# Normalising three of four query blocks' probabilities inside the transposing product

## The chip, the cores and the metric

The kernel runs on one core of one Trainium2 chip. The time is the device time in microseconds (us) of one execution. The kernel before took 2144.35 us (median of three runs, 2143.05 to 2144.57). The profile that is shown comes from one further execution, which took 2142.89 us and whose span, from its first to its last instruction, is 2141.1 us.

In the profile, PE is the matrix engine (TensorE), PEld its loading of the stationary operand, DVE the vector engine, ACT the scalar engine, POOL GpSimd and SP the engine that issues most DMAs. A name such as L855 is a line of the kernel before.

## The reference

Two layers, each with three token mixers that read the same normalised input of 1024 tokens: a gated delta rule, multi-head attention with latent projections, and a gated linear recurrence. The change lies in the attention alone, which is causal and swept over blocks of 128 queries, for 8 heads:

```python
def one_block(args):
    qi, i = args
    s = jnp.einsum('bhqd,bhkd->bhqk', qi, k).astype(jnp.float32) * scale
    qpos = i * Q_BLOCK + jnp.arange(Q_BLOCK)
    s = jnp.where(kpos[None, :] <= qpos[:, None], s, -jnp.inf)
    p = jax.nn.softmax(s, axis=-1).astype(v.dtype)
    return jnp.einsum('bhqk,bhkd->bhqd', p, v)
```

So each row of probabilities is exp(s - max) divided by its sum, and then multiplied with the values. All data are float32.

## The kernel before

Each layer has two stages. The first (`phase_a` and `lru`) holds the input projection and the two recurrent mixers. The second, `phase_c`, holds the attention and the projection of its output. Most products of the kernel are made of three single passes on operands that are split into a high and a low part of a rounded type (`mm3`, L132 to L136; the products at L805 to L809 and L866 to L868 are written out in the same manner). A few products, such as L392 and L379 of the first stage and the sums of squares at L209, work on unsplit float32 operands instead.

In `phase_c` each head's queries are taken in two halves (`sb` 0 and 1) of four blocks (`qi` 0 to 3). For each half two generators run:

- `attn_scores` forms for each query block the scores against all keys up to its own block, in one or two pieces of up to 512 keys (L805 to L809, in PSUM). DVE masks the diagonal block and takes the negative maximum (L815), ACT takes the exponential and its row sums (L823, recorded under the helper's L86) into a tile `P` of 512 or 1024 columns, DVE adds the sums and takes the reciprocal into `mx[:, 5:6]` (L826). Then the whole row of probabilities is multiplied by it: for `qi` 0 to 2 by POOL (the helper `gts`, L105), for `qi` 3 by DVE for the first 512 columns (L830) and by POOL for the other 512 in the second half.
- `attn_out` walks over the key blocks `kb`. For each it transposes the 128x128 blocks of the four (in the causal corner fewer) query blocks into one PSUM bank `tp` (L855), ACT rounds the bank into `th` (recorded as pth, L140) and DVE takes the rest `tl` (ptl, L141), and PE multiplies both with the values (L866 to L868). The products on one key block are issued after the transposes of the next one. There are two `tp` banks and two `th` and `tl` buffers.

The transposing is itself a product on PE: the block of `P` is the stationary operand and an identity matrix (`con`) the moving one. Counted over heads, halves and layers there are 576 of these: (10 + 26) per head, times 8 heads and 2 layers. Of them 384 belong to `qi` 0 to 2 (6 in the first half of a head, 18 in the second) and 192 to `qi` 3 (4 and 8).

The order of the work in `phase_c` is set in two steps: a list `todo` of generator steps with due times (in units of one half of a head), which puts a half's `attn_out` one unit after its `attn_scores` with a lag of 0.1, and mixes projections in between; and then the framework's scheduler, which orders each engine's queue by priority and its own estimate of durations. Engines then work through their queues in order.

Of the kernel before, what the change touches and what calls it, by code (L numbers as in the profile page):

```python
# [63 lines left out]
class Trunk:  # L64
# [718 lines left out]
    def attn_scores(self, h, sb, q, qr, k, P):  # L783

        nc, pc, con = self.nc, self.pc, self.con
        qh, ql = q[sb]
        qr = qr[h % 2]
        for qi in range(4):
            qb = sb * 4 + qi
            qs = slice(qi * 128, qi * 128 + 128)  # L790
            w = 128 * (qb + 1)

            pieces = [(0, w)] if w <= H2 else [(0, H2), (H2, w)]
            n = len(pieces)
            mx = pc.tile([128, 8], F32, name="mx", tag="mx", bufs=6)
            S = []
            for j, (k0, k1) in enumerate(pieces):
                ps = self.pb.tile([128, H2], F32, name="pS", tag="S")
                a = k0
                while a < k1:  # L800
                    e = min(k1, (a // H2 + 1) * H2)
                    kh, kl = k[a // H2]
                    ks = slice(a % H2, (e - 1) % H2 + 1)
                    out = ps[:, a - k0 : e - k0]
                    nc.tensor.matmul(out, qh[:, qs], kh[:, ks], start=True, stop=False)  # L805
                    nc.tensor.matmul(out, qh[:, qs], kl[:, ks], start=False, stop=False)
                    nc.tensor.matmul(out, ql[:, qs], kh[:, ks], start=False, stop=False)
                    nc.tensor.matmul(out, qr[sb][:, qs], self.kp[:, a:e], start=False, stop=False)
                    nc.tensor.matmul(out, qr[sb][:, qs], self.kl[:, a:e], start=False, stop=True)  # L809
                    a = e  # L810
                if j == n - 1:
                    dg = ps[:, k1 - k0 - 128 : k1 - k0]
                    self.tt(dg, dg, con[:, K_CAUS : K_CAUS + 128], ALU.add)
                S.append(ps[:, : k1 - k0])
                nc.vector.tensor_reduce(mx[:, j : j + 1], S[j], AX.X, ALU.max, negate=True)  # L815
            sc = self.scq[:, qb : qb + 1]
            if n == 2:
                nc.vector.tensor_scalar(mx[:, 2:3], mx[:, 0:1], mx[:, 1:2], sc, ALU.min, ALU.mult)  # L818
            else:
                nc.vector.tensor_scalar(mx[:, 2:3], mx[:, 0:1], sc, None, ALU.mult)  # L820
            pt = self.pp.tile([128, 512 * (sb + 1)], F32, name="P", tag=f"P{2 * (sb + 1)}", bufs=4)
            for j, (k0, k1) in enumerate(pieces):
                self.act(pt[:, k0:k1], S[j], AF.Exp, scale=sc, bias=mx[:, 2:3], accum_out=mx[:, 3 + j : 4 + j])  # L823
            if n == 2:
                nc.vector.tensor_scalar(mx[:, 3:4], mx[:, 3:4], mx[:, 4:5], None, ALU.add)
            nc.vector.reciprocal(mx[:, 5:6], mx[:, 3:4])  # L826
            if qi == 3:

                w0 = pieces[0][1]
                nc.vector.tensor_scalar(pt[:, :w0], pt[:, :w0], mx[:, 5:6], None, ALU.mult)  # L830
                if n == 2:
                    self.gts(pt[:, w0:w], pt[:, w0:w], mx[:, 5:6])
            else:
                self.gts(pt[:, :w], pt[:, :w], mx[:, 5:6])
            P.append(pt)
            yield

    def attn_out(self, h, sb, P, V, ops):

        nc, pc = self.nc, self.pc  # L840
        if sb == 0:
            ops.extend(pc.tile([128, T], F32R, name="o", tag="ob", bufs=6) for _ in range(2))
        oh, ol = ops
        s = slice(sb * H2, (sb + 1) * H2)
        mz = pc.tile([128, H2], F32, name="mz", tag="mzh", bufs=1)
        nc.sync.dma_start(mz, self.mzd[h][:, s])
        po = self.bank("po")
        nkb = 4 * sb + 4
        prev = None
        for kb in range(nkb + 1):  # L850
            if kb < nkb:
                q0 = max(0, kb - 4 * sb)
                tp = self.bank("tp")
                for qi in range(q0, 4):
                    nc.tensor.transpose(tp[:, qi * 128 : qi * 128 + 128], P[qi][:, kb * 128 : kb * 128 + 128], self.ident)  # L855
                th = pc.tile([128, H2], F32R, name="pth", tag="pth", bufs=2)
                tl = pc.tile([128, H2], F32R, name="ptl", tag="ptl", bufs=2)
                w = slice(q0 * 128, H2)
                self.split(th[:, w], tl[:, w], tp[:, w])
                here = (kb, w, th, tl)  # L860
            if prev:
                j, w, th, tl = prev
                vh, vl = V[j // 2]
                v0 = (j % 2) * 256 + (h % 2) * 128
                vs = slice(v0, v0 + 128)
                nc.tensor.matmul(po[:, w], vh[:, vs], th[:, w], start=(j == 0), stop=False)  # L866
                nc.tensor.matmul(po[:, w], vl[:, vs], th[:, w], start=False, stop=False)
                nc.tensor.matmul(po[:, w], vh[:, vs], tl[:, w], start=False, stop=(j == nkb - 1))  # L868
            prev = here
            if kb < nkb:  # L870
                yield
        self.gate_split(po, 0.5, mz, oh[:, s], ol[:, s], nc.gpsimd)
# [376 lines left out]
```

## Time and profile before

| | |
|---|---|
| median of three runs | 2144.35 us |
| the profiled execution | 2142.89 us |
| its span | 2141.1 us |
| PE busy | 2052.8 us, 96% of the span |
| PE's weight loads (PEld) busy | 1686.7 us, 79% |
| DVE, ACT, POOL busy | 60%, 39%, 32% |
| attention of the first layer, about | 700 to 1040 us |
| attention of the second layer, about | 1755 to 2100 us |
| transposes of P (L855), 576 records | 98.6 us busy |
| POOL's normalising of P (L105), 112 instructions | 80.3 us busy |

Busy times are unions of records, and PE's records overlap: a matmul's record ends well after the next one has started. What a matmul costs PE in a row of them is therefore read from the distance of starts and not from its own duration.

### The profile page before, as it was taken

Reading aid. Unit: us, or ns where it says so; the run is one execution under the profiler, and the core shown is the slowest. Engines: PE = TensorE matmul, PEld = TensorE weight load, DVE = VectorE, ACT = ScalarE, POOL = GpSimd, SP = SyncE. Lnnn points to the kernel's source line nnn. Section 1 sums busy time; section 2 is a strip of 40 time slices with the busy share of each in tenths; the row PEclk is TensorE's granted clock in tenths of the full one; section 3 lists DMA queues with packets and bytes.
Section 4 is the critical chain, followed back from the end, with each engine's and each line's share of the span. In section 5 each row is a group of like instructions: output and inputs, shape, how many; then the busy total and the mean of one; then the engine's idle time right before and its main releaser. Section 6 shows DMA issues by size and latency. Waiting matters only on the chain.

```text
span 2141.1 us, 28752 instructions
## 1 busy us (share of the span) xinstructions
PE 2052.8 (96%) x10380; PEld 1686.7 (79%) x10380; DVE 1289.3 (60%) x2530; ACT 841.9 (39%) x1759; POOL 676.6 (32%) x752
## 2 busy tenths in 40 slices
PE   7999999999999999999899999999999989999997
PEld 4888878787777788888678888787877878888875
DVE  6556546544831777676754575474458237776766
ACT  5241243144720554443542313432366125444534
POOL 2132332233241433332332223333223423332322
PEclk9999999999999999999999999999999999999999
DMA  5123113414143015335511321134232520335263
GB/s 176 55 81 116 55 50 104 123 55 143 45 173 131 25 50 177 110 119 180 189 54 40 114 86 52 60 104 133 69 108 79 177 92 24 110 119 164 65 216 123
DMA packets 135103, 222.08 MB, mean 104 GB/s; under 512 B 37808, under 2 KB 60336, under 8 KB 134960
## 3 DMA queue, kind: packets, MB, share of 16 engines
q1 hardware_dynamic: 134960, 220.24, 31.6%
q8 instruction: 82, 1.34, 0.3%
q14 instruction: 61, 0.50, 0.1%
HBM read 147.31 MB, written 72.88 MB: 103 GB/s over the span
## 4 chain that ended last, share of the span: by engine, by line
PE 83%; DVE 6%; ACT 4%; DMA 3%; issue 2%; POOL 2%; SPq 0%; DVEq 0%; POOLq 0%; ACTq 0%
PE pbig L136 12%; PE pbig L135 12%; PE pbig L132 12%; PE pspj L132 4%; PE pspj L135 4%; PE pspj L136 4%; PE pspr L135 3%; PE pspr L136 3%; PE pspr L132 3%; PE pstp L855 2%; PE pspo L868 2%; PE pspo L866 2%; PE pssc L494 1%; PE pssc L498 1%; PE pS L805 1%
## 5 line engine op out<-in xcount | busy, mean ns | idle before, releaser
L123 POOL TENSOR_TENSOR wlo<-wst,whi 128x1024 fp32r<-128x1024 f32 (+3 forms) x196 | 325.1, 1660 | 922.2 <-DVE whi L122 323.6
L132 PE MATMUL pbig<-h,whi 128*128 128x512 f32 x1216 | 485.1, 399 | 5.4 <-ACT h L140 3.6
L136 PE MATMUL pbig<-h,wlo 128*128 128x512 f32 x1216 | 484.7, 399 | 4.4 <-POOL wlo L123 4.4
L135 PE MATMUL pbig<-h,whi 128*128 128x512 f32 x1216 | 483.9, 398 | 2.2 <-DVE h L141 2.2
L132 PEld LDWEIGHTS pbig<-h,whi 128*128 128x128 f32 x1216 | 230.3, 189 | 51.1 <-ACT h L140 4.7
L136 PEld LDWEIGHTS pbig<-h,wlo 128*128 128x128 f32 x1216 | 230.5, 190 | 50.6 <-POOL wlo L123 6.2
L135 PEld LDWEIGHTS pbig<-h,whi 128*128 128x128 f32 x1216 | 230.6, 190 | 46.8 <-DVE h L141 2.9
L86 ACT ACTIVATE P<-pS,mx,scq 128x512 f32<-128x512 f32 (+1 forms) x192 | 128.0, 669 | 151.5 <-DVE mx L818 78.8
L122 DVE CAST whi<-wst 128x1024 fp32r<-128x1024 f32 x92 | 70.1, 762 | 191.8 <-PE pbig L135 140.9
L105 POOL TENSOR_SCALAR P<-P,mx 128x128 f32<-128x128 f32 (+6 forms) x112 | 80.3, 718 | 206.9 <-DVE mx L826 106.9
L140 ACT CAST pth<-pstp 128x512 fp32r<-128x512 f32 x192 | 90.6, 478 | 80.4 <-PE pstp L855 79.0
L120 ACT CAST whi<-wst 128x256 fp32r<-128x256 f32 (+2 forms) x104 | 46.5, 448 | 189.3 <-DMA wst<-in_w_uk 100.8
L815 DVE TENSOR_REDUCE mx<-pS 128x1 f32<-128x512 f32 (+1 forms) x192 | 106.6, 555 | 17.5 <-PE pS L809 11.3
L141 DVE TENSOR_TENSOR ptl<-pstp,pth 128x512 fp32r<-128x512 f32 x192 | 105.0, 552 | 14.7 <-ACT pth L140 14.3
L855 PE MATMUL pstp<-con,P 128*128 128x128 f32 x576 | 98.6, 276 | 6.1 <-DVE P L830 5.3
L102 DVE TENSOR_TENSOR xt<-pspj,xt 128x512 f32<-128x512 f32 x96 | 66.3, 690 | 51.1 <-PE pspj L136 23.7
L855 PEld LDWEIGHTS pstp<-con,P 128*128 128x128 f32 x576 | 72.5, 142 | 25.4 <-DVE P L830 7.1
L132 PE MATMUL pspj<-lh,whi 128*128 128x512 f32 x208 | 84.7, 407 | 5.4 <-ACT whi L120 5.2
L135 PE MATMUL pspj<-ll,whi 128*128 128x512 f32 x208 | 82.3, 396 | 0.0
L866 PE MATMUL pspo<-pth,vh 128*128 128x512 f32 x192 | 79.6, 415 | 2.6 <-ACT pth L140 2.5
L136 PE MATMUL pspj<-lh,wlo 128*128 128x512 f32 x208 | 82.0, 394 | 0.1
L86 ACT ACTIVATE z<-pbig 128x1024 f32<-128x1024 f32 x24 | 24.6, 1026 | 145.6 <-PE pbig L136 145.6
(276 smaller groups left out, 4520.7 us busy)
## 6 DMA issues: line engine op xcount, KB each, us to landing
wst<-in_w_in SPq DMA_DIRECT2D x76, 512.0 KB, 3.6
x<-xt SPq DMA_DIRECT2D x128, 256.0 KB, 3.4
xt<-x SPq DMA_DIRECT2D x112, 256.0 KB, 3.5
mzd<-z SPq DMA_DIRECT2D x16, 512.0 KB, 4.5
wst<-in_w_o SPq DMA_DIRECT2D x16, 512.0 KB, 3.5
mz<-mzd SPq DMA_DIRECT2D x32, 256.0 KB, 2.9
wst<-in_w_o SPq DMA_DIRECT2D x64, 128.0 KB, 2.1
xk<-x SPq DMA_DIRECT2D x32, 256.0 KB, 4.5
```

The lines of the kernel that those rows point to most:

```text
L86: return self.nc.scalar.activation(out, in_, func, **kw)
L105: self.nc.gpsimd.tensor_scalar(out, a, s, 1.0, ALU.mult, ALU.mult)
L122: nc.vector.tensor_copy(hi[:, :n], st[:, :n])
L123: (eng or nc.gpsimd).tensor_tensor(lo[:, :n], st[:, :n], hi[:, :n].bitcast(F32), ALU.subtract)
L132: first = nc.tensor.matmul(out, ah, bh, start=(start and j == 0), stop=False)
L135: nc.tensor.matmul(out, ah, bl, start=False, stop=False)
L136: nc.tensor.matmul(out, al, bh, start=False, stop=(stop and j == n - 1))
L140: self.nc.scalar.copy(hi, x)
L141: (eng or self.nc.vector).tensor_tensor(lo, x, hi.bitcast(F32), ALU.subtract)
L815: nc.vector.tensor_reduce(mx[:, j : j + 1], S[j], AX.X, ALU.max, negate=True)
L855: nc.tensor.transpose(tp[:, qi * 128 : qi * 128 + 128], P[qi][:, kb * 128 : kb * 128 + 128], self.ident)
L866: nc.tensor.matmul(po[:, w], vh[:, vs], th[:, w], start=(j == 0), stop=False)
```

## The change

For `qi` 0 to 2 the row of probabilities is no longer multiplied by the reciprocals. Instead POOL multiplies the 128x128 identity by them, which gives a diagonal matrix `dg`; it is stored in the last 128 columns of the same tile `P`, which these query blocks do not use. `attn_out` then uses `dg` in the place of the identity for these blocks: the product of the transposed block with the diagonal matrix is transposed and normalised at once. It is issued as an ordinary product and no longer as a transpose. `qi` 3, whose row fills the tile, is left as it was.

```diff
@@ attn_scores
                 nc.vector.tensor_scalar(pt[:, :w0], pt[:, :w0], mx[:, 5:6], None, ALU.mult)
                 if n == 2:
                     self.gts(pt[:, w0:w], pt[:, w0:w], mx[:, 5:6])
+                P.append((pt, self.ident))
             else:
-                self.gts(pt[:, :w], pt[:, :w], mx[:, 5:6])
-            P.append(pt)
+
+                dg = pt[:, 512 * sb + 384 :]
+                self.gts(dg, self.ident, mx[:, 5:6])
+                P.append((pt, dg))
             yield
@@ attn_out
                 tp = self.bank("tp")
                 for qi in range(q0, 4):
-                    nc.tensor.transpose(tp[:, qi * 128 : qi * 128 + 128], P[qi][:, kb * 128 : kb * 128 + 128], self.ident)
+                    p, dg = P[qi]
+                    out = tp[:, qi * 128 : qi * 128 + 128]
+                    if qi == 3:
+                        nc.tensor.transpose(out, p[:, kb * 128 : kb * 128 + 128], dg)
+                    else:
+                        nc.tensor.matmul(out, p[:, kb * 128 : kb * 128 + 128], dg, start=True, stop=True)
```

On PE's queue the first half of a head, at its second and third key block, shows the exchange. L855 is the transpose before; afterwards L863 is the product with the diagonal and L861 the transpose that is left; L866 to L868 become L874 to L876. An operation is one row here, whatever number of instructions it is made of. Before:

```order
L136 MATMUL pspj<-lh,wlo 128x512
L855 MATMUL pstp<-con,P 128x128 x3
L866 MATMUL pspo<-pth,vh 128x512
L867 MATMUL pspo<-pth,vl 128x512
L868 MATMUL pspo<-ptl,vh 128x512
L855 MATMUL pstp<-con,P 128x128 x2
L805 MATMUL pS<-k,q 128x512
L806 MATMUL pS<-k,q 128x512
L807 MATMUL pS<-k,q 128x512
L808 MATMUL pS<-kp,qr 128x512
L866 MATMUL pspo<-pth,vh 128x384
```

And now:

```order
L136 MATMUL pspj<-lh,wlo 128x512
L863 MATMUL pstp<-P 128x128 x2
L861 MATMUL pstp<-con,P 128x128
L874 MATMUL pspo<-pth,vh 128x512
L875 MATMUL pspo<-pth,vl 128x512
L876 MATMUL pspo<-ptl,vh 128x512
L863 MATMUL pstp<-P 128x128
L861 MATMUL pstp<-con,P 128x128
L805 MATMUL pS<-k,q 128x512
L806 MATMUL pS<-k,q 128x512
L807 MATMUL pS<-k,q 128x512
L874 MATMUL pspo<-pth,vh 128x384
```

The number of operations is the same, two of three (one of two) transposes have become products, and one score product (L808) has changed places with the products on the values.

On POOL's queue the first two halves of the first head read before (w is 128, 256, 384 and then 640, 768, 896 columns; wlo is the low part of a weight, o the low part of a head's output):

```order
L105 TENSOR_SCALAR P<-P,mx 128x128
L105 TENSOR_SCALAR P<-P,mx 128x256
L105 TENSOR_SCALAR P<-P,mx 128x384
L123 TENSOR_TENSOR wlo<-wst,whi 128x384
L105 TENSOR_SCALAR P<-P,mx 128x640
L123 TENSOR_TENSOR wlo<-wst,whi 128x384
L105 TENSOR_SCALAR P<-P,mx 128x768
L105 TENSOR_SCALAR P<-P,mx 128x896
L141 TENSOR_TENSOR o<-of,o 128x512
L105 TENSOR_SCALAR P<-P,mx 128x512
```

And now:

```order
L105 TENSOR_SCALAR P<-con,mx 128x128 x3
L123 TENSOR_TENSOR wlo<-wst,whi 128x384
L105 TENSOR_SCALAR P<-con,mx 128x128
L123 TENSOR_TENSOR wlo<-wst,whi 128x384
L105 TENSOR_SCALAR P<-con,mx 128x128 x2
L141 TENSOR_TENSOR o<-of,o 128x512
L105 TENSOR_SCALAR P<-P,mx 128x512
```

The places are the same and the six instructions per head are all 128 columns wide; the one on 512 columns (`qi` 3) is left.

## The prediction

> **What bounds the kernel now.** I read the page's busy shares first, then the shares of the chain of work that ended last.
>
> ```profile
> span 2141.1 us, 28752 instructions
> PE 2052.8 (96%) x10380; PEld 1686.7 (79%) x10380; DVE 1289.3 (60%) x2530; ACT 841.9 (39%) x1759; POOL 676.6 (32%) x752
> PE 83%; DVE 6%; ACT 4%; DMA 3%; issue 2%; POOL 2%; SPq 0%; DVEq 0%; POOLq 0%; ACTq 0%
> ```
>
> PE is busy nearly throughout and makes 83% of the chain; POOL, which the change relieves, makes 2%. An average says little of one stage, so next the busy time by stretch, for the two stretches in which the attention runs (columns: length, then busy time and count for PE, PEld, DVE, ACT and POOL, granted clock, DMA share, GB/s).
>
> ```profile
> 700.00:1040.00 340.00, 328.24 (x1773) 275.39 (x1774) 243.92 (x574) 165.07 (x403) 116.09 (x130) 1.00 0.36 118
> 1755.00:2100.00 345.00, 334.13 (x1793) 280.37 (x1794) 245.13 (x577) 167.04 (x408) 114.22 (x128) 0.99 0.36 116
> ```
>
> There too PE sets the time: it is idle for 340.00 - 328.24 = 11.8 us in the first and 345.00 - 334.13 = 10.9 us in the second stretch, 22.6 us together, at a full clock. POOL is busy for a third. So whatever is added to PE's queue lengthens the kernel, except where it fills those 22.6 us; and what is taken from POOL is worth only what PE waits for POOL. The list of waits tells what the idle time is (first stretch; the second has the same eight rows within 0.4 us each).
>
> ```profile
> PE pstp L855 <- DVE P L830: 2.7, 3, 0.9
> PE pspo L868 <- DVE ptl L141: 2.3, 4, 0.8
> PE pS L805 <- ACT P L86: 2.1, 4, 1.4
> PE pS L808 <- DVE qr L102: 1.4, 1, 1.4
> PE pspo L866 <- ACT pth L140: 1.3, 1, 1.3
> PE pspj L132 <- DVE k L141: 1.2, 2, 1.0
> PE pspj L135 <- POOL o L141: 0.8, 1, 0.8
> PE pstp L855 <- POOL P L105: 0.4, 2, 0.2
> ```
>
> The wait that the change shortens directly, transposes for POOL's normalising, is the last row: 0.4 us. The larger wait for P is for DVE's L830, which normalises query block 3 and stays as it is.
>
> **What is added on PE.** 384 of the 576 transposes become ordinary products of two float32 128x128 operands. The trace of before has such products, though not on this data: L392 in the first stage, 64 of them in the code (4 groups of 4, for 2 pairs of heads and 2 layers). The groups of instructions say how they run:
>
> ```profile
> L855 PE MATMUL pstp<-con,P 128*128 128x128 f32 x576 | 98.6, 276 | 6.1 <-DVE P L830 5.3 <-POOL P L105 0.8
> L392 PE MATMUL pspr<-kT 128*128 128x128 f32 x128 | 17.0, 276 | 0.0
> L392 PEld LDWEIGHTS pspr<-kT 128*128 128x128 f32 x128 | 15.7, 191 | 0.5 <-DVE a L99 0.3
> ```
>
> 576 transposes have 576 records; 64 products have 128, and 128 weight loads. So a product of unsplit float32 operands is issued as two matmuls, a transpose as one. The mean durations are equal (276 ns), but records overlap; the price is the distance of starts in the timeline (start, length of the row, then the group):
>
> ```profile
> 744.10 0.60 PE L855 MATMUL pstp<-con,P 128*128 128x128 f32 x4
> 744.45 0.48 PE L805 MATMUL pS<-k,q 128*128 128x512 f32 x1
> 744.77 0.40 PE L806 MATMUL pS<-k,q 128*128 128x512 f32 x1
> 745.00 0.40 PE L807 MATMUL pS<-k,q 128*128 128x512 f32 x1
> ...
> 134.44 0.39 PE L136 MATMUL pbig<-h,wlo 128*128 128x512 f32 x1
> 134.67 1.05 PE L392 MATMUL pspr<-kT 128*128 128x128 f32 x8
> 135.48 0.48 PE L132 MATMUL pbig<-h,whi 128*128 128x512 f32 x1
> 135.79 0.40 PE L135 MATMUL pbig<-h,whi 128*128 128x512 f32 x1
> ```
>
> Four transposes: 744.45 - 744.10 = 0.35 us, and the product behind them takes 0.32 until the next start where its neighbour takes 0.23, so 0.09 more: 0.44 us for four, 0.11 each. Four products (eight records): 135.48 - 134.67 = 0.81, and behind them 0.31 where 0.23 is usual: 0.89 for four, 0.2225 each. The difference is 0.1125 us, and 384 x 0.1125 = **+43.2 us**.
>
> The Trainium skill has a rule that speaks against this change more strongly: its page "TensorE: Matmul & The Clock Gate", section "Terms", says that the transposing mode is four times faster for FP32. By it a product would take 4 x 0.11 = 0.44 us and the change would add 384 x 0.33 = 127 us, an estimate from that page's factor. The rows above do not agree: they show a factor of two for this size, and the sum goes by them.
>
> A cost that no row shows is the change from product to transpose within one bank: 160 banks hold both (3 in a head's first half, 7 in its second, for 8 heads and 2 layers). The nearest rows are plain products of one column followed by transposes in the first stage:
>
> ```profile
> 116.82 1.94 PE L322 MATMUL pspr<-ep,th 128*128 128x1 f32 x16
> 118.61 0.63 PE L344 MATMUL pspr<-con,kT 128*128 128x128 f32 x4
> ...
> L322 PE MATMUL pspr<-ep,th 128*128 128x1 f32 x128 | 15.1, 248 | 0.0
> ```
>
> The last of the 16 starts at 116.82 + 1.94 - 0.25 = 118.51, the transpose 0.10 later: no more than the usual distance. So I take 0; the upper end is another 0.09 such as stands behind each group now, 160 x 0.09 = +14 us; the lower end is 0, since nothing there could be gained.
>
> **What is taken from POOL.** Seven sizes are normalised now, sixteen times each:
>
> ```profile
> L105 POOL TENSOR_SCALAR P<-P,mx 128x896 f32<-128x896 f32 x16 | 16.3, 1016 | 39.6 <-DVE mx L826 18.7 <-ACT k L140 14.7 <-ACT o L140 6.3
> L105 POOL TENSOR_SCALAR P<-P,mx 128x768 f32<-128x768 f32 x16 | 14.6, 909 | 12.2 <-PE pS L809 4.5 <-DVE pS L102 3.0 <-ACT q L140 2.5
> L105 POOL TENSOR_SCALAR P<-P,mx 128x640 f32<-128x640 f32 x16 | 12.8, 801 | 24.4 <-ACT q L140 14.5 <-DVE mx L826 9.9
> L105 POOL TENSOR_SCALAR P<-P,mx 128x384 f32<-128x384 f32 x16 | 9.4, 586 | 35.7 <-DVE mx L826 34.8
> L105 POOL TENSOR_SCALAR P<-P,mx 128x256 f32<-128x256 f32 x16 | 7.7, 478 | 42.7 <-DVE mx L826 32.9 <-PE pstp L855 5.1 <-PE pspj L136 4.7
> L105 POOL TENSOR_SCALAR P<-P,mx 128x128 f32<-128x128 f32 x16 | 5.9, 372 | 5.8 <-DVE mx L826 5.8
> ```
>
> These six together are 66.7 us. Afterwards they are 96 instructions of 128 columns at 0.372, 35.7 us: POOL is relieved by 31 us (the seventh, 512 columns, stays). What of it reaches the end: the waits for POOL's P, 0.4 in each stretch, and two places near the ends of the stretches, where the chain itself runs through POOL:
>
> ```profile
> 1032.76 1.01 POOL P L105
> 1033.77 1.26 POOL o L141
> 1035.08 0.50 PE pspj L135
> ...
> 2089.31 1.01 POOL P L105
> ```
>
> There the 896 columns stand ahead of the low part of an output for which PE waits: 1.016 - 0.372 = 0.64 us each time. Together 0.8 + 1.3 = about -2 us; at most -3.7, with all waits for POOL's o (0.8 per stretch) gone as well; at least 0. All of this is idle time of PE, so it is a part of the 22.6 us and not additional.
>
> **What the idle time swallows.** ACT and DVE have no more work than before, and PE reaches their results later. Between the transposes of a key block and the products on it stand the transposes of the next block, now longer by up to 3 x 0.1125 = 0.34 us. The waits for pth and ptl are 0.4 to 1.3 us long on average by the rows above (2.3 us in 4, 1.3 in 1), so such a delay takes a part of each, and the same holds for the waits for DVE's P and for the score banks (L805). Waits for a projection (qr, k) have nothing to do with it and may stay. The ends are 0 and -22.6; I take half, **-11 us**, with POOL's 2 in it. If this cover is gone, the full 43.2 shows.
>
> Queues other than PE's get almost no new order: as the rows on the change show, POOL's places are the same, and on PE a score product changes places with products on values. I cost that at nothing, since both stand in a queue that is full anyway.
>
> **Sum.** +43.2 + 0 - 11 = +32 us. Against the profiled execution (2142.89 us, span 2141.1) this is 2175 us; the median of the runs is 1.5 us above that execution, so the forecast is **2176 us**.
>
> **Rivals.**
>
> *Nothing is swallowed and the mixture costs something.* The transposed bank is complete 0.34 us later, so ACT's cast and DVE's subtraction start later; where only the next transposes cover them, the wait is not shortened but moved. For it: the order of the bank's chain (PE, ACT, DVE, PE) is unchanged. Against it: the following bank's transposes are longer as well. Time: +43.2 to +43.2 + 14, 2188 to 2202, say 2194.
>
> *More is swallowed than the idle time shows.* Records of 0.27 us at distances of 0.11 hide stalls below some 0.16 us, which then count as busy. An estimate of ten more us, about 5 us in each stretch, gives 43.2 - 22.6 - 10 = +11: 2155 (2152 to 2165). For it: the many short rows; against it: the distances in the timeline are regular.
>
> *Weight loads that don't hide.* A product needs two loads of 191 ns each (row L392 PEld). If the next stationary block could not be loaded ahead because blocks and diagonals alternate, a product would take 0.38 us and the change 384 x (0.38 - 0.11) = +104, less 11 swallowed: 2237. Against it: in L392 the stationary block changes as well from product to product, and eight records took 0.81 us. The factor of four of the Trainium skill's page would lie here too.
>
> *The other side: the product runs as one record.* If a product with the diagonal were issued like a transpose, PE's queue would be as long as before and only POOL's relief would be left: -3.7 at most, 2141, no change or a little faster. It decides as soon as the records of L863 number 384 instead of 768. Against it: L392's 128 records for 64 products, and nothing in the change asks for a transpose.
>
> **Chances.** Forecast (2165 to 2188, from all of the idle time filled to none) 0.66; nothing swallowed 0.16; more swallowed 0.10; loads not hidden 0.03; one record 0.03; anything else, such as the moved rows, 0.02. A measurement of this kernel tells about 0.2%, 4.3 us, from no change. All cases but the one-record one, and half of the rest, are slower by more: slower 0.96, within 0.2% 0.02, faster 0.02. The range for 8 in 10 is 2158 to 2198: the forecast's own, about two thirds of the case above and half of the one below.
>
> **What would show it.** In the changed kernel's profile L863 should have 768 records with 768 loads, in rows of six records 0.11 us apart; PE's busy time in the attention should grow by some 20 us per layer and its share stay at 97% or rise; POOL's P instructions should be 96 at 0.37 us beside 16 of 512 columns; the waits of L874, L876 and L805 should have shrunk by about a third to a half, while L830's product still holds up some transposes. The first stage (0 to about 690 us) should be unchanged to 1 us. The prediction is wrong if L863 has 384 records, if starts of its records lie 0.19 us apart, or if PE's idle time in the attention grows.

## The result, and the profile after

The changed kernel takes 2176.61 us (median of four runs, 2175.2 to 2176.81) beside 2143.7 us for the kernel before (median of the four runs made with it). The ratio is 1.0152, with a 95% interval of 1.0138 to 1.0167: slower by 1.5%, about 33 us. The profiled execution took 2176.48 us with a span of 2174.6 us. The page of it:

```profile
span 2174.6 us, 29471 instructions
PE 2088.6 (96%) x10764; PEld 1730.5 (80%) x10764; DVE 1296.2 (60%) x2530; ACT 844.2 (39%) x1759; POOL 640.8 (29%) x752
PE 30%; DVE 3%; ACT 2%; DMA 2%; issue 1%; POOL 1%; DVEq 0%; SPq 0%; ACTq 0%; POOLq 0%
```

PE has 384 matmuls more than before and POOL is 36 us less busy, while DVE and ACT are as they were. The chain (last line) could be followed back over some 40% of the span only, so its shares are not to be compared with those of before.

The groups of instructions (count, then busy time, mean duration in ns, idle time before them and what ended it) show the exchange, and below it the products on the values of the changed kernel:

```profile
L863 PE MATMUL pstp<-P 128*128 128x128 f32 x768 | 113.4, 277 | 0.4 <-POOL P L105 0.4
L861 PE MATMUL pstp<-con,P 128*128 128x128 f32 x192 | 52.3, 276 | 8.5 <-DVE P L830 8.5
L863 PEld LDWEIGHTS pstp<-P 128*128 128x128 f32 x768 | 107.8, 192 | 10.8 <-POOL P L105 1.3
L105 POOL TENSOR_SCALAR P<-con,mx 128x128 f32<-128x128 f32 x96 | 36.4, 380 | 161.3 <-DVE mx L826 153.6
...
L874 PE MATMUL pspo<-pth,vh 128*128 128x512 f32 x96 | 45.8, 477 | 0.6 <-ACT pth L140 0.6
L876 PE MATMUL pspo<-ptl,vh 128*128 128x512 f32 x96 | 38.6, 403 | 0.0
L876 PE MATMUL pspo<-ptl,vh 128*128 128x384 f32 x32 | 11.3, 353 | 0.0
L805 PE MATMUL pS<-k,q 128*128 128x256 f32 x32 | 9.3, 291 | 5.5 <-ACT P L86 5.5
```

The same groups before:

```profile
L866 PE MATMUL pspo<-pth,vh 128*128 128x512 f32 x96 | 46.0, 479 | 2.5 <-ACT pth L140 2.5
L868 PE MATMUL pspo<-ptl,vh 128*128 128x512 f32 x96 | 39.8, 415 | 2.4 <-DVE ptl L141 2.4
L868 PE MATMUL pspo<-ptl,vh 128*128 128x384 f32 x32 | 11.8, 370 | 3.9 <-DVE ptl L141 3.9
L805 PE MATMUL pS<-k,q 128*128 128x256 f32 x32 | 9.5, 298 | 3.2 <-ACT P L86 3.2
```

The 384 products have 768 records and 768 loads of 192 ns. The waits for pth and ptl, 8.8 us in these three rows before, are 0.6 us. The wait for DVE's L830, 5.3 us before, is 8.5 us, and that for a score bank (L805) went from 3.2 to 5.5 us. How fast the records follow each other is in the timeline:

```profile
737.46 0.83 PE L863 MATMUL pstp<-P 128*128 128x128 f32 x6
738.13 0.27 PE L861 MATMUL pstp<-con,P 128*128 128x128 f32 x1
738.15 0.47 PE L874 MATMUL pspo<-pth,vh 128*128 128x512 f32 x1
738.47 0.40 PE L875 MATMUL pspo<-pth,vl 128*128 128x512 f32 x1
738.70 0.40 PE L876 MATMUL pspo<-ptl,vh 128*128 128x512 f32 x1
```

Three products take 738.13 - 737.46 = 0.67 us, 0.223 each. The transpose behind them takes 0.02 until the next start, and the product after it 0.32 instead of 0.23: 0.11 together, as before. Here nothing is lost between products and transpose.

Both attention stretches can be followed from the first to the last transposing instruction of a layer: 337.6 and 335.3 us before, 353.8 and 350.8 us after, +16.2 and +15.5. To see where it went, the time from each PE instruction's start to the next one's start was added up from the trace by what the instruction writes, over both stretches (us; a wait counts for the instruction ahead of it):

```
                     before   after   difference
transposing (tp)       61.9   108.1      +46.2
values (po)           130.8   119.3      -11.5
projections (pj)      309.8   308.0       -1.8
scores (S)            170.4   169.2       -1.2
sum                   672.9   704.6      +31.7
```

The remaining 1.8 us of the span's +33.5 lie outside. The first product of the attention's projections already starts 1.2 us later (685.6 for 684.4), and in other executions of this study 1.2 us earlier or 3.7 us later, although the order of the instructions ahead of it is the same. So a part outside the stretches that differs by a few us between two single executions says nothing about the change.

### The profile page after: what moved, and what is told of

Same layout as the page of the kernel before. It is cut to its first block, busy times and chain, and to the rows that moved or that the text cites. A ratio compares the mean times of both kernels' runs of the same rounds, so it can differ in the third digit from the quotient of the medians.

```text
span 2174.6 us, 29471 instructions
## 1 busy us (share of the span) xinstructions
PE 2088.6 (96%) x10764; PEld 1730.5 (80%) x10764; DVE 1296.2 (60%) x2530; ACT 844.2 (39%) x1759; POOL 640.8 (29%) x752
## 5 line engine op out<-in xcount | busy, mean ns | idle before, releaser
L123 POOL TENSOR_TENSOR wlo<-wst,whi 128x1024 fp32r<-128x1024 f32 (+3 forms) x196 | 319.7, 1632 | 976.2 <-DVE whi L122 323.1
L141 DVE TENSOR_TENSOR ptl<-pstp,pth 128x512 fp32r<-128x512 f32 x192 | 105.3, 555 | 35.6 <-ACT pth L140 32.6
L815 DVE TENSOR_REDUCE mx<-pS 128x1 f32<-128x512 f32 (+1 forms) x192 | 106.6, 555 | 18.3 <-PE pS L809 11.6
L863 PEld LDWEIGHTS pstp<-P 128*128 128x128 f32 x768 | 107.8, 192 | 10.8 <-POOL P L105 1.3
L863 PE MATMUL pstp<-P 128*128 128x128 f32 x768 | 113.4, 277 | 0.4 <-POOL P L105 0.4
L105 POOL TENSOR_SCALAR P<-con,mx 128x128 f32<-128x128 f32 x96 | 36.4, 380 | 161.3 <-DVE mx L826 153.6
L874 PE MATMUL pspo<-pth,vh 128*128 128x512 f32 x192 | 79.0, 411 | 1.6 <-ACT pth L140 1.4
```

What stands on the lines that cost most here:

```text
L123: (eng or nc.gpsimd).tensor_tensor(lo[:, :n], st[:, :n], hi[:, :n].bitcast(F32), ALU.subtract)
L141: (eng or self.nc.vector).tensor_tensor(lo, x, hi.bitcast(F32), ALU.subtract)
L863: nc.tensor.matmul(out, p[:, kb * 128 : kb * 128 + 128], dg, start=True, stop=True)
```

## The experiments

Stretch sums of the experiments are made in the same way as in the table above. The kernel before took 2143.8, 2144.9 and 2145.1 us in the three groups of runs (the first four kernels, the next four, the last two); each ratio is to the kernel before in the same group.

### How many products: 224, 384 and 576

The product alone, with the identity in place of the diagonal and the normalising left as it was; N is 2, 3 or 4:

```diff
-                    nc.tensor.transpose(tp[:, qi * 128 : qi * 128 + 128], P[qi][:, kb * 128 : kb * 128 + 128], self.ident)
+                    out = tp[:, qi * 128 : qi * 128 + 128]
+                    if qi < N:
+                        nc.tensor.matmul(out, P[qi][:, kb * 128 : kb * 128 + 128], self.ident, start=True, stop=True)
+                    else:
+                        nc.tensor.transpose(out, P[qi][:, kb * 128 : kb * 128 + 128], self.ident)
```

> Query blocks 0 and 1 alone (224 of the 576) are transposed by an ordinary product with the identity; normalising stays as in the kernel before. My theory (a product costs PE 0.1125 us more than a transpose, and about a quarter of it is swallowed by PE's idle time): 224 x 0.1125 = +25 less 6, so +19 us, and 448 records for them. Rival 1 (the change's cost comes from waiting for the diagonals or from the other way of normalising): within 5 us of before. Rival 2 (the change from product to transpose within a bank costs): 128 banks are mixed here against 160 in the change, so the rise would be near 128/160 of the change's +33, +26 us.

> The change's 384 products, but with the identity in place of the diagonal, and the normalising as before: the product alone, without POOL's relief. My theory: +43 on PE less 9 swallowed, +34 us, a little above the change itself (+33), by the 2 us of POOL's relief. Rival 1 (diagonals or normalising make the cost): within 5 us of before. Rival 3 (POOL's relief was worth far more, some 10 us, and the product costs its whole price): +43 us.

> All 576 transposes become products with the identity; normalising as before; no bank is mixed. My theory: 576 x 0.1125 = +65 less a quarter at most, +49 to +55 us. Rival 2 (mixing products and transposes in a bank costs): no more than the change, near +33 us or below it, since no bank is mixed. If what is swallowed stays at 11 us whatever the number of products: +54.

Measured: 224 products 2171.38 us, ratio 1.0128 (1.0114 to 1.0142), +27 us; 384 products 2176.2 us, 1.0152 (1.0133 to 1.0172), +33 us; 576 products 2193.79 us, 1.0225 (1.0201 to 1.025), +48 us. The first is 8 us above what I expected, the other two are as expected within their intervals, and a rise of 43 us for 384 products with no relief of POOL (rival 3) is excluded. The 384 products with the identity cost what the change costs, so neither the diagonals nor the new way of normalising is the cause (rival 1). The +27 us of 224 products are what rival 2 gave (+26), so that run alone would speak for a cost of mixing. The run of 576 decides: without any mixed bank the rise is half as large again as the change's, so mixing is not the cause (rival 2).

The groups of the transposing instructions, for 224, 384 and 576 products in this order:

```profile
L859 PE MATMUL pstp<-con,P 128*128 128x128 f32 x352 | 72.5, 276 | 10.4 <-DVE P L830 9.9 <-POOL P L105 0.4
L857 PE MATMUL pstp<-con,P 128*128 128x128 f32 x448 | 72.1, 277 | 0.0
```

```profile
L857 PE MATMUL pstp<-con,P 128*128 128x128 f32 x768 | 114.2, 278 | 0.6 <-POOL P L105 0.4
L859 PE MATMUL pstp<-con,P 128*128 128x128 f32 x192 | 52.5, 277 | 8.5 <-DVE P L830 8.5
```

```profile
L857 PE MATMUL pstp<-con,P 128*128 128x128 f32 x1152 | 164.4, 277 | 8.9 <-DVE P L830 8.8
```

Every product has two records, and in each kernel the wait for L830 is above the 5.3 us of before. The stretch sums, read together with PE's idle time, give the price of a product over a transpose and what came back of it (us). In these sums idle time counts for the instruction ahead of it; the price is the rise of the transposing instructions' sum (tp) without the idle time in it. "PE's idle time" is how all of it in the two stretches changed (21.6 us before). "The rest" is how the other sums (values, scores, projections) changed without their idle time:

```
                 tp sum  idle in it  price  per product   PE's idle time  the rest   rise
before             61.9     10.4
224 products       93.4     16.9      25.0     0.112           +2.2          -3.1    +24.1
384 products      109.1     12.2      45.4     0.118           -6.4          -7.5    +31.5
the change        108.1     12.5      44.1     0.115           -4.7          -7.8    +31.7
576 products      128.7     11.2      66.0     0.115           -6.9         -12.7    +46.5
```

So the price on PE is proportional to the number, 0.11 to 0.12 us, while what comes back is not. With 224 products it is 0.9 us: the time on the values falls by 8 us, but the waits for L830 grow by nearly 5, and PE's idle time as a whole rises; the other 3 us of the +27 lie outside of the stretches. Here the step "about a quarter is swallowed" failed. With 384 it is 12 to 14 us and with 576 some 20, of which only 5 to 7 were idle time before.

### POOL's part alone

```diff
+                P.append((pt, self.ident))
             else:
-                self.gts(pt[:, :w], pt[:, :w], mx[:, 5:6])
-            P.append(pt)
+                dg = pt[:, 512 * sb + 384 :]
+                self.gts(dg, self.ident, mx[:, 5:6])
+                P.append((pt, dg))
@@ attn_out
-                    nc.tensor.transpose(tp[:, qi * 128 : qi * 128 + 128], P[qi][:, kb * 128 : kb * 128 + 128], self.ident)
+                    p, dg = P[qi]
+                    out = tp[:, qi * 128 : qi * 128 + 128]
+                    nc.tensor.transpose(out, p[:, kb * 128 : kb * 128 + 128], self.ident)
```

> POOL's part alone: query blocks 0 to 2 are not normalised at all (POOL still makes the diagonals, and nothing reads them), and all 576 stay transposes with the identity, so the output leaves the division for these blocks out. My theory: POOL is off the path, -2 us, at most -4. Rival 3 (POOL's relief is worth some 10 us, and without it the change would have cost 43): -10 us.

Measured: 2143.25 us, ratio 1.0001 (0.999 to 1.0012), that is -2 to +3 us. POOL's relief is worth nothing that can be measured; -10 us is excluded, and my -2 is at the edge of the interval.

### The kind of instruction or the number

```diff
-                    nc.tensor.transpose(tp[:, qi * 128 : qi * 128 + 128], P[qi][:, kb * 128 : kb * 128 + 128], self.ident)
+                    for _ in range(2 if qi < 3 else 1):
+                        nc.tensor.transpose(tp[:, qi * 128 : qi * 128 + 128], P[qi][:, kb * 128 : kb * 128 + 128], self.ident)
```

> The kernel before, with each of the 384 transposes of query blocks 0 to 2 issued twice into the same place; no ordinary product. It separates the kind of instruction from its number. My theory (the change costs the second record, whatever kind it is): 384 x 0.11 = +42 less the 11 us that the waits for pth and ptl give back, +31 us, the same as the change within 4 us. Rival (the ordinary product costs by its own: its loads of 191 instead of 140 ns, or mixing with transposes): clearly less than the change, +20 us or below.

Measured: 2183.68 us, ratio 1.019 (1.0166 to 1.0215), +41 us (+36 to +46).

```profile
L856 PE MATMUL pstp<-con,P 128*128 128x128 f32 x960 | 141.1, 275 | 9.1 <-DVE P L830 8.9
```

The transposing instructions take 108.9 us in the two stretches, near the change's 108.1: without the idle time in them (13.8 us, 10.4 before) the price is 43.6 for 384 more, 0.114 each. So a second transpose costs PE what the product's second record costs; the kind of instruction makes no difference to the price. The whole is some 7 us above the change, outside of the 4 us that I allowed. Of the 6.3 us between the two profiled spans (2180.9 and 2174.6), 2.6 lie inside the stretches (707.2 for 704.6, with 123.4 for 119.3 on the values and less on the projections) and 3.7 outside of them. There the order of PE's instructions is the same but for a few at the edges, and the part between the two attentions takes 719.9 us for the change's 716.8, as it takes 715.1 to 721.2 in other profiled executions. Why the medians lie 7 us apart stays open. The rival (a product dear by its own, +20 us or less here) is excluded.

### All four blocks with a diagonal

```diff
             if qi == 3:
-                w0 = pieces[0][1]
-                nc.vector.tensor_scalar(pt[:, :w0], pt[:, :w0], mx[:, 5:6], None, ALU.mult)
-                if n == 2:
-                    self.gts(pt[:, w0:w], pt[:, w0:w], mx[:, 5:6])
+                dg = P[0][0][:, 512 * sb + 128 : 512 * sb + 256]
             else:
-                self.gts(pt[:, :w], pt[:, :w], mx[:, 5:6])
-            P.append(pt)
+                dg = pt[:, 512 * sb + 384 :]
+            self.gts(dg, self.ident, mx[:, 5:6])
+            P.append((pt, dg))
@@ attn_out
-                    nc.tensor.transpose(tp[:, qi * 128 : qi * 128 + 128], P[qi][:, kb * 128 : kb * 128 + 128], self.ident)
+                    p, dg = P[qi]
+                    out = tp[:, qi * 128 : qi * 128 + 128]
+                    nc.tensor.matmul(out, p[:, kb * 128 : kb * 128 + 128], dg, start=True, stop=True)
```

> Query block 3 gets a diagonal too (kept in unused columns of the tile of block 0), so all 576 are products, and DVE's normalising at L830 and POOL's of 512 columns are gone. My theory: the +50 of 576 products with the identity, less the waits for L830 that those still had (5.3 us visible in the first layer, 9 to 10 in both): +40 to +45 us. Rival (those waits only move to the diagonal of block 3 on POOL): +50 us.

Measured: 2191.51 us, ratio 1.0223 (1.0205 to 1.0242), +48 us (+44 to +52).

```profile
L854 PE MATMUL pstp<-P 128*128 128x128 f32 x1152 | 164.2, 277 | 8.5 <-POOL P L105 8.5
```

My expectation failed, though the interval's lower end just reaches it. The wait for L830 did not go with L830: it is now as long (8.5 us for 8.8) for the diagonal of block 3 on POOL. The rows do not say more than that PE comes to block 3 before its sums are there; the last instruction of that chain, on whichever engine, is named as the one waited for.

### L830 cut in two

In the kernel before, and in the changed kernel:

```diff
-                nc.vector.tensor_scalar(pt[:, :w0], pt[:, :w0], mx[:, 5:6], None, ALU.mult)
+                for c0, c1 in ((0, 128), (128, w0)):
+                    nc.vector.tensor_scalar(pt[:, c0:c1], pt[:, c0:c1], mx[:, 5:6], None, ALU.mult)
```

> The kernel before, with DVE's normalising of block 3 (L830) cut in two: 128 columns first, the rest behind. The first transpose could then start after a shorter instruction. My theory: eight recurring waits for L830 of 0.2 to 0.9 us each get some 0.25 us shorter, -2 us, near what can be measured; 32 more DVE instructions are off the path. Rival (DVE's queue is what PE waits for): 0 to +3 us.

> The same cut in the changed kernel, where the waits for L830 are longer (1.2 us each at seven places): -2 to -3 us against the change's 2176.6, so 2174. Rival: no difference to the change, 2176 to 2178.

Measured: 2150.61 us, ratio 1.0028 (1.0015 to 1.0041), +6 us; and 2184.99 us, 1.0189 (1.0169 to 1.0208), 8 us above the change. Both expectations failed on the slow side, and the timeline of the first shows a reason: an uncontended piece of 384 columns (713.27), the two pieces at a place where POOL is at work, and POOL at that place.

```profile
713.27 0.42 DVE L831 TENSOR_SCALAR P<-P,mx 128x384 f32<-128x384 f32 x1
...
765.95 0.28 DVE L831 TENSOR_SCALAR P<-P,mx 128x128 f32<-128x128 f32 x1
766.15 0.68 DVE L141 TENSOR_TENSOR k<-pspj,k 128x512 fp32r<-128x512 f32 x1
766.75 1.53 DVE L831 TENSOR_SCALAR P<-P,mx 128x384 f32<-128x384 f32 x1
768.20 0.29 DVE L102 TENSOR_TENSOR pS<-pS,con 128x128 f32<-128x128 f32 x1
```

```profile
766.09 0.71 POOL L105 TENSOR_SCALAR P<-P,mx 128x512 f32<-128x512 f32 x1 [1.25 <-ACT k L140]
766.76 1.30 POOL L141 TENSOR_TENSOR o<-of,o 128x512 fp32r<-128x512 f32 x1
```

The second piece comes while POOL is at work and ends 0.22 us after POOL's next instruction has ended (768.28 for 768.06): 1.53 us instead of 0.42, and all of DVE's queue stands behind it. This is no single place. Of the 32 second pieces 18 take 0.41 to 0.42 us. The other 14 come during an instruction of POOL and take 0.9 us (one), 1.5 (twelve) and 2.5 (one). Two of the 18 overlap one of POOL as well; there it is POOL's that takes longer (1.01 us for 0.70). All pieces together take 39.0 us, where the 32 uncut instructions took 16.4. PE's products on the values come behind these places, and their waits grow (before, then with the cut):

```profile
PE pspo L866 <- ACT pth L140: 2.5, 2, 1.3
...
PE pspo L867 <- ACT pth L140: 5.2, 8, 1.2
```

In the two stretches PE takes 9.4 us more than before (682.4 for 672.9). In the changed kernel the same line takes 40.7 us cut and 18.3 uncut. A few instructions of PE and DVE have also changed places, and what part that has in the loss was not tried.

### The splits first

```diff
-                self.split(th[:, w], tl[:, w], tp[:, w])
+                with self.prio(-self.LOW):
+                    self.split(th[:, w], tl[:, w], tp[:, w])
```

> The kernel before, with the casts and subtractions that make pth and ptl given priority in ACT's and DVE's queues (only the order of the queues changes). It tests what the change's extra time on PE was swallowed by. My theory: the products on the values (L866 to L868) lost some 11 us to waits for pth and ptl; with the splits first a good part of this goes without any product with a diagonal, -5 to -10 us, 2134 to 2139, unless the softmax chain, now behind them, gives back as much. Rival (the swallowed time is not that wait, or priority only moves it): -2 to +5 us.

> The same priority in the changed kernel. My theory: here those waits are gone already, so the priority gains nothing (0 to +3 us against the change), and the distance to the kernel before with splits first is nearer the full price of 384 products, +40 to +46 us. Rival: the distance stays +32 us.

Measured: 2142.17 us, ratio 0.9985 (0.9973 to 0.9997), -3 us; and 2174.53 us, 1.0142 (1.0115 to 1.0169). The distance between the two is 32 us (2174.53 - 2142.17), the rival's number; by the two intervals it is known to some 6 us, so that 40 is just outside. Both expectations failed: of the time on the values only 3 us went (127.9 for 130.8), and other waits rose:

```profile
L855 PE MATMUL pstp<-con,P 128*128 128x128 f32 x576 | 98.5, 276 | 7.8 <-DVE P L830 6.7 <-POOL P L105 1.1
L869 PE MATMUL pspo<-ptl,vh 128*128 128x384 f32 x32 | 11.7, 366 | 0.3
L805 PE MATMUL pS<-k,q 128*128 128x256 f32 x32 | 9.7, 302 | 5.5 <-ACT P L86 5.3
```

The waits for ptl are nearly gone (3.9 to 0.3 us in the row of 384 columns), and the waits for the softmax (L830, L805), now behind the splits in ACT's and DVE's queues, grew from 5.3 to 6.7 and from 3.2 to 5.5 us. So priority moves a wait from one chain to the other: PE's idle time in the stretches is 21.6 us as before. This version is the only one whose interval lies below the kernel before; it ends just under 1, and the gain of 0.15% is less than what I counted as a difference.

## Why the prediction was right

**What bounds the kernel.** PE, as read. From the first to the last transposing instruction of each layer, before and then now:

```profile
713.81:1051.42 337.61, 325.54 (x1736) 271.66 (x1736) 240.79 (x559) 162.09 (x396) 113.73 (x124) 0.99 0.38 125
1768.41:2103.73 335.32, 325.81 (x1734) 272.60 (x1734) 237.37 (x557) 162.34 (x397) 108.50 (x122) 0.99 0.37 118
...
715.24:1069.03 353.79, 344.69 (x1925) 295.85 (x1925) 241.06 (x558) 163.29 (x395) 98.76 (x124) 1.00 0.37 120
1785.79:2136.61 350.82, 343.00 (x1925) 294.44 (x1925) 237.93 (x557) 163.33 (x397) 93.55 (x122) 1.00 0.35 113
```

PE is idle for 12.1 and 9.5 us before (3.6% and 2.8%), and for 9.1 and 7.8 us now (2.6% and 2.2%). Its busy time grows by 19.2 and 17.2 us, near the 20 per layer of the prediction.

**The price of a product: +43.2 us.** Right in every part: two records, two loads, 0.223 us per product, 44.1 us for all when the idle time is taken off, proportional from 224 to 576 products, and the same for repeated transposes. The rule of the Trainium skill ("TensorE: Matmul & The Clock Gate", section "Terms") that the transposing mode is four times faster for FP32 does not agree with this size either: the factor here is 0.223 to 0.11, two.

**Mixing in a bank: 0.** Right; the transpose behind three products costs its usual 0.11 us, and the kernel with no mixed bank is not cheaper per product (0.115 us in both).

**POOL's relief: -2 us.** Not to be told from nothing (-2 to +3 us with POOL's part alone).

**What the idle time swallows: -11 us.** The number came out, the mechanism only in part, and that the two agree is luck. Between the price of 44.1 us and the rise of 31.7 in the stretches lie 12.4 us, near the 11 that the prediction took as half of 22.6 without a reason for the half. But PE's idle time fell by 4.7 us only, from 21.6 to 16.9. The waits for pth and ptl, from which the prediction took a part, went nearly whole (8.8 to 0.6 us in the three rows above). The waits for DVE's L830 and for the score banks, which it counted among those that shrink, rose from 5.3 to 8.5 and from 3.2 to 5.5 us (L805, 256 columns). The other 7.8 us came out of time that the profile counts as busy, which the prediction put at nothing. A part of that can be waits that no row shows: a record of 0.40 us with the next start 0.23 us behind it (L875 in the timeline above) covers the first 0.17 us of a wait. A part can be the new order of the queue. Which part is which is not shown.

Of the 3.2 us more for L830, 1.44 us are one place, which was not there before:

```profile
1055.76 1.95 DVE L830 TENSOR_SCALAR P<-P,mx 128x512 f32<-128x512 f32 x1
...
1055.05 2.37 POOL L123 TENSOR_TENSOR wlo<-wst,whi 128x1024 fp32r<-128x1024 f32 x1 [3.71 <-DVE whi L122]
...
1057.76 0.33 PE L861 MATMUL pstp<-con,P 128*128 128x128 f32 x1 [1.44 <-DVE P L830]
```

DVE's instruction comes during POOL's weight of the next stage and ends when that has ended. The rest are six places, one in each of the first three pairs of heads in both layers, that waited 0.89 us and now 1.18 (first one shown, after):

```profile
763.95 0.69 DVE L141 TENSOR_TENSOR q<-pspj,q 128x512 fp32r<-128x512 f32 x1 [1.72 <-ACT q L140]
...
765.87 0.68 DVE L815 TENSOR_REDUCE mx<-pS 128x1 f32<-128x512 f32 x1
...
770.48 0.33 PE L861 MATMUL pstp<-con,P 128*128 128x128 f32 x1 [1.18 <-DVE P L830]
```

There PE comes to block 3 before its maximum and sums are through DVE and ACT. In this example DVE now takes the maximum (765.87) 2.4 us after the end of the block's first score products (763.46), where it was 1.2 us before (761.75 after 760.56). Ahead of the maximum in DVE's queue stand q's subtraction, which had to wait for ACT, then sums, a piece of ptl and k's subtraction. PE comes later too, so that only 0.29 us of this is left as a wait. What part of it the order makes was not tried.

**The first stage.** The first product of the attention's projections starts 1.2 us later than before, where the prediction allowed 1 us; executions with the same order up to there differ by more.

**The rivals.** "Nothing is swallowed and the mixture costs" is out by the 12.4 us between the price and the rise and by the unmixed kernel. "More is swallowed than the idle time shows" is out as a time (2155 us), but its premise, that more than the idle time can give way, is what the 7.8 us look like; it had all of the idle time filled as well, and of that only 4.7 us went. "Loads that don't hide" and "one record" are out by 768 records at 0.112 us; whether the transposing mode itself could take the diagonal was not tried. What stays open is how much of the return is truly cover and how much is the new order of the queues.

## What to carry to other kernels

On an engine that is busy for 97% of a stage, count the records of the new instruction in a place where the kernel already runs it, and price it by the distance of starts, not by its duration: 276 and 277 ns stood here for 0.11 and 0.223 us. Work that is taken from an engine off the path is worth no more than the waits for it, here 0.4 us per layer. Expect a part of an addition to PE to fill waits for its followers, but not evenly: the waits for a chain that ends at PE's next operand can grow while others vanish. And the idle time on the page is neither what will be filled nor the bound of it, since overlapping records can count short waits as busy: here 4.7 us of 21.6 went, and 7.8 us came from time that counted as busy.

## What the runs showed of the hardware

A DVE instruction on SBUF alone (the product of P and the reciprocals, one tensor in) can be held for the whole of a POOL instruction. 384 columns took 0.42 us alone and 1.53 us where they came during POOL's L105 and L141, and 512 columns took 1.95 us during POOL's L123 of 2.37 us, instead of 0.49. POOL is held in the same way: its L105 of 512 columns takes 0.69 us in six places of the kernel before, and 0.91 in seven where DVE's L830 had begun 0.14 us earlier. This is what the Trainium skill describes on its page "SBUF — State Buffer", section "SBUF: two separate sides": the port pair that the two engines share is locked for a whole instruction, by one of GpSimd or by one of DVE that runs in a two-port mode or has two inputs in SBUF, and the one that comes second waits. The trace agrees in these places as to the waiting; in which mode DVE's instruction ran, no row shows. I had not priced it. The cut that should have gained 2 us lost 6, and the 14 held pieces are the reason that the traces show for it.
